# A chain of 3001 GpSimd memsets beside a residual-add and RMSNorm kernel

## The chip, the cores and the metric

The kernel runs on one core of one Trainium2 chip. The metric is the device time of one execution in microseconds (us); lower is better. The median of several is given with its lowest and highest value. The engines are called as the profile calls them: DVE is VectorE, ACT is ScalarE, POOL is GpSimd, SP is SyncE. SPq and ACTq are the queues on which SP and ACT issue transfers.

## The reference

```python
def reference(x, residual, gamma, eps):          # x, residual: (32, 2048, 2048) float32
    z = x + residual
    rms = np.sqrt(np.mean(z ** 2, axis=-1, keepdims=True) + eps)
    return (z / rms * gamma).astype(np.float32)
```

There are 65536 rows of 2048 numbers. Both inputs are read once and the result is written once: 3 x 537 MB = 1611 MB.

## The kernel before

A tile is 7 rows on each of 128 partitions (7168 KB). There are two buffers `z` (x comes in, and the result goes out of the same place) and one area for the residual. Work is spread so: SP loads x and writes the result, ACT loads the residual and sums the squares, DVE adds and scales. GpSimd has nothing to do but the final waits.

```python
    def sp_turn(sp, t):                      # SyncE, one turn
        t.wait(sp, "done", -1)               # the scale of tile i-1 has ended
        inc(sp.dma_start(out=rows(o_f, i - 1), in_=z[(i - 1) % 2]...), "s_out", i - 1)
        ...
        t.wait(sp, "s_out", -1)              # that result has landed: its buffer is free
        ...
            load_x(sp, t, 1)                 # x of tile i+1 into the same buffer

    def dve_turn(v, t, own):                 # VectorE, one turn
        t.wait(v, "x_in"); t.wait(v, "r_in")
        inc(add(v, i, a0, b0), "add_a", i)   # z <- z + r_area, both in SBUF: 128x6144
        inc(add(v, i, a1, b1), "add_b", i)   #                                128x8192
        for h, (a, b) in enumerate(parts(i)):
            ...                              # reciprocal of the rms, after ACT
            ins = scale(v, i, a, b, rstd[p][h])   # z <- z * rstd * gamma_tile (PSUM)
        inc(ins, "done", i)
    ...
    nc.gpsimd.wait_ge(ev["s_out"][(last - 1) % 2], ((last - 1) // 2 + 1) * U)
    nc.gpsimd.wait_ge(s_tail, U * len(tail))
    ...                                      # then GpSimd clears the semaphores
```

(Lines with "..." are cut, and two waits are drawn onto one line.)

Of the kernel before, what the change touches and what calls it, by code (L numbers as in the profile page):

```python
# [9 lines left out]
def kernel(  # L10
# [17 lines left out]
    nc = tc.nc  # L28
    P = nc.NUM_PARTITIONS
# [35 lines left out]
    def sb(name, shape):  # L65
        return ctx.enter_context(nc.sbuf_tensor(name, shape, fp32))
# [6 lines left out]
    def sem(name):  # L73
        sems.append(ctx.enter_context(nc.semaphore(name)))
        return sems[-1]
# [6 lines left out]
    ssq = [[sb(f"ssq{p}{h}", [P, 4]) for h in range(2)] for p in range(2)]  # L82
    rms = [[sb(f"rms{p}{h}", [P, 4]) for h in range(2)] for p in range(2)]
    rstd = [[sb(f"rstd{p}{h}", [P, 4]) for h in range(2)] for p in range(2)]
    tail_ssq = sb("tail_ssq", [P, R])
    tail_rms = sb("tail_rms", [P, R])
    tail_rstd = sb("tail_rstd", [P, R])
# [8 lines left out]
    dve = sem("dve_own")  # L96
    act = sem("act_own")
    s_tail = sem("s_tail")
    tail_ev = {k: sem(f"tail_{k}") for k in ("add", "rms", "done")}


# [115 lines left out]
    def act_part(s, chain, src, a, b, sq, rm):  # L217

        for g in range(a, b):
            if g > a:  # L220
                chain.wait()
            chain.next(
                s.activation(  # L223
                    out=sq_junk[:, :],
                    in_=src[:, g, :],
                    func=Act.Square,
                    accum_out=sq[:, g - a : g - a + 1],
                )
            )
        chain.wait()  # L230
        return s.activation(  # L231
            out=rm, in_=sq[:, : b - a], func=Act.Sqrt, bias=eps_tile[:, :], scale=inv_d
        )

    def act_turn(s, t, chain):
        i, p = t.i, t.p
        for h, (a, b) in enumerate(parts(i)):
            chain.wait()
            t.wait(s, "add_a" if h == 0 else "add_b")
            if h == 0 and i > 0:  # L240
                load_r(s, t, 1)
            inc(
                act_part(s, chain, z[p], a, b, ssq[p][h], rms[p][h][:, : b - a]),
                "rms_a" if h == 0 else "rms_b",
                i,
            )
# [26 lines left out]
    def vector_program(v):  # L273
        v.memset(eps_tile[:, :], float(eps))  # L274
        v.memset(stage, 0.0).then_inc(tail_ev["add"], 1)  # L275
        v.wait_ge(g_in, 4 * U)
        v.stream_shuffle(gamma_tile[:, :].rearrange("p (a b) -> p a b", a=16), stage, [0] * 32)  # L277
        for i in range(LO):
            dve_turn(v, Turn(i), lambda i, h: (2 * i + h + 1) * U)
        with v.Fori(0, 2 * n_iter, 2) as it:  # L280
            for i in range(LO, LO + 2):
                dve_turn(v, Turn(i, it), lambda i, h: it * (2 * U) + (2 * i + h + 1) * U)
        for i in range(HI, last):
            dve_turn(v, Turn(i), lambda i, h: (2 * i + h + 1) * U)
        base = 2 * last * U
        t = Turn(last)
        t.wait(v, "r_in")

        def tail_scale(k):
            a, b = tail[k]  # L290
            v.wait_ge(tail_ev["rms"], k + 1)
            v.reciprocal(out=tail_rstd[:, a:b], in_=tail_rms[:, a:b]).then_inc(dve, U)  # L292
            v.wait_ge(dve, base + (k + 1) * U)
            scale(v, last, a, b, tail_rstd, a).then_inc(tail_ev["done"], 1)

        for k, (a, b) in enumerate(tail):
            v.wait_ge(x_tail[k], U)
            add(v, last, a, b).then_inc(tail_ev["add"], 1)
            if k:
                tail_scale(k - 1)  # L300
        tail_scale(len(tail) - 1)

    def scalar_program(s):
        chain = Chain(s, act)
        for i in range(LO):
            act_turn(s, Turn(i), chain)
        with s.Fori(0, 2 * (n_iter - 1), 2) as it:
            n = chain.n
            chain.base = it * R
            for i in range(LO, LO + 2):  # L310
                act_turn(s, Turn(i, it), chain)
            assert chain.n - n == 2 * R
        chain.base = None
        chain.n = n + 2 * R * (n_iter - 1)
        for i in range(HI - 2, last):
            act_turn(s, Turn(i), chain)
        for k, (a, b) in enumerate(tail):
            chain.wait()
            s.wait_ge(tail_ev["add"], k + 2)
            act_part(  # L320
                s, chain, z[last % 2], a, b, tail_ssq[:, a:b], tail_rms[:, a:b]
            ).then_inc(tail_ev["rms"], 1)

    sync_program(nc.sync)
    vector_program(nc.vector)
    scalar_program(nc.scalar)

    nc.gpsimd.wait_ge(ev["s_out"][(last - 1) % 2], ((last - 1) // 2 + 1) * U)
    nc.gpsimd.wait_ge(s_tail, U * len(tail))
# [38 lines left out]
```

## Time and profile before

| | before |
|---|---|
| time, median of 4 (lowest to highest) | 3724.94 us (3724.76 to 3725.41) |
| transfers | 1610.68 MB, 433 GB/s, DMA engines full |
| DVE, ACT, POOL busy | 62%, 29%, 0% |
| one steady turn (one tile) | 50.8 us |

The groups of instructions, kept apart by shape, give the durations that the argument needs. The columns are line, engine, operation, shapes and count, then total busy us and mean ns of one, then the idle time of the engine before them and what ended it:

```profile
L177 DVE SCALAR_TENSOR_TENSOR z<-z,rstd,gamma_tile 128x2048 f32<-128x2048 f32 x505 | 1153.6, 2344 | 5.2
...
L172 DVE TENSOR_TENSOR z<-z,r_area 128x8192 f32<-128x8192 f32 x72 | 625.3, 8685 | 0.0
L172 DVE TENSOR_TENSOR z<-z,r_area 128x6144 f32<-128x6144 f32 x71 | 465.6, 6558 | 1242.4 <-DMA z<-in_x_dram 1242.4
```

The reader is to see that an add of the larger part takes 8685 ns, that the scales hardly wait, and that DVE's 1242 us of idle time lie where x has not landed yet. The rest of the reading of this profile is in the prediction.

### The profile page before, as it was taken

The numbers are of one execution on the slowest core, as the hardware profiler recorded it, in microseconds if no ns is written. First come the engines' busy times: TensorE is split into PE (matmuls) and PEld (weight loads), VectorE is DVE, ScalarE is ACT, GpSimd is POOL, SyncE is SP. The second block draws the span as 40 slices with busy tenths as digits, with TensorE's granted clock in tenths as the row PEclk, the third lists the DMA queues.
The fourth block names the chain that finished last, engine by engine and source line by source line (L and its number), as shares of the span: only waits on it lengthen the run. The fifth ranks groups of instructions, "written<-read, shape, count | busy, mean of one in ns | idle before, by whom it ended". The sixth has DMA issues, their size and how long they took to land.

```text
span 3723.7 us, 3798 instructions
## 1 busy us (share of the span) xinstructions
DVE 2302.6 (62%) x816; ACT 1072.4 (29%) x1176; POOL 0.2 (0%) x4
## 2 busy tenths in 40 slices
DVE  5666665566665566665566665566665566665566
ACT  2233322233322233322233322233322233322233
POOL 0000000000000000000000000000000000000000
DMA  9999999999999999999999999999999999999999
GB/s 421 431 434 435 434 434 435 434 435 435 434 434 434 434 434 434 434 434 433 434 434 434 434 434 434 434 434 434 434 434 434 434 434 434 434 434 434 434 432 398
DMA packets 32963, 1610.68 MB, mean 433 GB/s; under 512 B 3712, under 2 KB 3776, under 8 KB 3776
## 3 DMA queue, kind: packets, MB, share of 16 engines
q1 hardware_dynamic: 22592, 1082.17, 67.2%
q10 hardware_dynamic: 10368, 528.49, 32.8%
q14 instruction: 3, 0.02, 0.0%
HBM read 1073.77 MB, written 536.87 MB: 433 GB/s over the span
## 4 chain that ended last, share of the span: by engine, by line
DMA 67%; DVE 22%; issue 9%; ACT 2%; SPq 0%; DVEq 0%; ACTq 0%
DMA out_dram<-z 39%; DMA z<-in_x_dram 27%; DVE z L172 15%; DVE z L177 7%; ACT sq_junk L223 1%; ACT rms L231 0%; DVE rstd L197 0%; SPq L259 0%; DVEq L127 0%; DVE r_area L275 0%; ACTq L211 0%; ACTq L127 0%; SPq L141 0%; DVE tail_rstd L292 0%; SPq L162 0%
## 5 line engine op out<-in xcount | busy, mean ns | idle before, releaser
L172 DVE TENSOR_TENSOR z<-z,r_area 128x8192 f32<-128x8192 f32 (+2 forms) x150 | 1109.5, 7437 | 1252.5 <-DMA z<-in_x_dram 1252.5
L223 ACT ACTIVATE sq_junk<-z 128x2048 f32<-128x2048 f32 x512 | 963.4, 1882 | 2617.1 <-DVE z L172 2605.7
L177 DVE SCALAR_TENSOR_TENSOR z<-z,rstd,gamma_tile 128x2048 f32<-128x2048 f32 x505 | 1153.6, 2344 | 5.2
L197 DVE RECIPROCAL rstd<-rms 128x4 f32<-128x4 f32 (+2 forms) x146 | 25.3, 173 | 130.8 <-ACT rms L231 130.8
L223 ACT ACTIVATION_READ_ACCUMULATOR sq_junk<-z 128x1 f32 x512 | 95.5, 186 | 0.0
L231 ACT ACTIVATE rms<-ssq,eps_tile 128x4 f32<-128x4 f32 (+2 forms) x146 | 43.3, 297 | 13.4
L177 DVE SCALAR_TENSOR_TENSOR z<-z,tail_rstd,gamma_tile 128x2048 f32<-128x2048 f32 x7 | 16.2, 2345 | 0.1
L277 DVE LOAD_MASK_SELECT gamma_tile<-r_area x1 | 0.0, 14 | 16.1 <-DMA r_area<-in_gamma_dram 16.1
L277 DVE STREAM_SHUFFLE gamma_tile<-r_area 128x2048 f32<-128x2048 f32 x1 | 2.3, 2290 | 0.0
L275 DVE MEMSET r_area<- 128x2048 f32 x1 | 1.8, 1765 | 0.4 <-issue 0.4
L223 ACT ACT_TABLE_LOAD x1 | 1.3, 1283 | 0.9 <-SPq L77 0.9
L231 ACT ACT_TABLE_LOAD x1 | 1.3, 1283 | 0.1
L231 ACT ACTIVATE tail_rms<-tail_ssq,eps_tile 128x2 f32<-128x2 f32 (+1 forms) x4 | 1.2, 295 | 0.1
L274 DVE MEMSET eps_tile<- 128x1 f32 x1 | 0.1, 59 | 1.0 <-SPq L77 1.0
L292 DVE RECIPROCAL tail_rstd<-tail_rms 128x2 f32<-128x2 f32 (+1 forms) x4 | 0.6, 158 | 0.0
L349 POOL MEMSET const-bfloat16-1.0<- 128x1 bf16 x1 | 0.1, 101 | 0.0
L349 POOL MEMSET const-uint8-127<- 128x1 uint8 x1 | 0.1, 101 | 0.0
L349 POOL MEMSET const-float32-0.0<- 128x1 f32 x1 | 0.1, 98 | 0.2 <-issue 0.2
L349 POOL MEMSET const-float32-1.0<- 128x1 f32 x1 | 0.1, 98 | 0.0
## 6 DMA issues: line engine op xcount, KB each, us to landing
r_area<-in_residual_dram ACTq DMA_DIRECT2D x72, 7168.0 KB, 35.5
z<-in_x_dram SPq DMA_DIRECT2D x71, 7168.0 KB, 27.5
out_dram<-z SPq DMA_DIRECT2D x71, 7168.0 KB, 40.8
z<-in_x_dram SPq DMA_DIRECT2D x3, 2048.0 KB, 17.9
out_dram<-z SPq DMA_DIRECT2D x3, 2048.0 KB, 15.0
r_area<-in_residual_dram SPq DMA_DIRECT2D x1, 5120.0 KB, 25.0
z<-in_x_dram SPq DMA_DIRECT2D x1, 5120.0 KB, 36.7
out_dram<-z SPq DMA_DIRECT2D x1, 5120.0 KB, 26.5
```

The costliest lines, as they stand in the source:

```text
L172: return v.tensor_add(out=s, in0=s, in1=r_area[:, e + a : e + b, :])
L177: ins = v.scalar_tensor_tensor(out=s, in0=s, scalar=rs[:, c + g - a : c + g - a + 1], in1=gamma_tile[:, :], op0=mult, op1=mult,)
L197: v.reciprocal(out=rstd[p][h][:, :n], in_=rms[p][h][:, :n]).then_inc(dve, U)
L223: s.activation(out=sq_junk[:, :], in_=src[:, g, :], func=Act.Square, accum_out=sq[:, g - a : g - a + 1],)
L231: return s.activation(out=rm, in_=sq[:, : b - a], func=Act.Sqrt, bias=eps_tile[:, :], scale=inv_d)
L274: v.memset(eps_tile[:, :], float(eps))
L275: v.memset(stage, 0.0).then_inc(tail_ev["add"], 1)
L277: v.stream_shuffle(gamma_tile[:, :].rearrange("p (a b) -> p a b", a=16), stage, [0] * 32)
L292: v.reciprocal(out=tail_rstd[:, a:b], in_=tail_rms[:, a:b]).then_inc(dve, U)
L349: nc = _bacc.Bacc("TRN2", target_bir_lowering=False, num_devices=1)
```

## The change

It gives GpSimd work that nothing needs. The intent is to learn what a busy GpSimd does to a kernel that does not use it. Every memset waits for the one before it.

```diff
+    scratch = sb("scratch", [P, 1024])
...
+    pool = sem("pool_own")
...
     scalar_program(nc.scalar)
+    nc.gpsimd.memset(scratch[:, :], 0.0).then_inc(pool, 1)
+    with nc.gpsimd.Fori(0, 3000, 8) as it:
+        for k in range(8):
+            nc.gpsimd.wait_ge(pool, it + (k + 1))
+            nc.gpsimd.memset(scratch[:, :], 0.0).then_inc(pool, 1)
+    nc.gpsimd.wait_ge(pool, 3001)
 
     nc.gpsimd.wait_ge(ev["s_out"][(last - 1) % 2], ((last - 1) // 2 + 1) * U)
```

## The prediction

> **What bounds the kernel now.** I read the page's engine shares and slices first, then the chain that ended last, then the timeline of one steady turn, then the GpSimd rows.
>
> The top of the page says that no compute engine is full and the transfers are:
>
> ```profile
> DVE 2302.6 (62%) x816; ACT 1072.4 (29%) x1176; POOL 0.2 (0%) x4
> ...
> DMA  9999999999999999999999999999999999999999
> ...
> DMA packets 32963, 1610.68 MB, mean 433 GB/s; under 512 B 3712, under 2 KB 3776, under 8 KB 3776
> ```
>
> The reader is to see three things: GpSimd (POOL) works 0.2 us, VectorE (DVE) 62% and the 16 DMA engines are at nine tenths or more in every slice. 1610.68 MB at 433 GB/s is 3720 us, the whole span of 3723.7. The stretches view of two steady turns makes it exact:
>
> ```profile
> core 0: us, DVE busy (x) ACT busy (x) POOL busy (x), PEclk, DMA share, GB/s
> 1909.43:1960.24 50.81, 31.41 (x11) 14.61 (x16) 0.00 (x0) 1.00 1.00 433
> 1960.24:2011.06 50.82, 31.41 (x11) 14.61 (x16) 0.00 (x0) 1.00 1.00 433
> ```
>
> The second 1.00 is the DMA share: full. One turn is one tile of three 7168 KB transfers (x in, residual in, result out): 3 x 7.34 MB = 22.02 MB at 433 GB/s = 50.8 us, just what the turn takes. VectorE works 31.4 us of it.
>
> The chain view of the same turns shows what the transfers wait for:
>
> ```profile
> 1891.84 40.80 DMA out_dram<-z
> 1932.66 27.51 DMA z<-in_x_dram
> 1960.24 15.17 DVE z L172 x2
> ```
>
> A result goes out of buffer z (40.8 us), the next x comes into it (27.5), then VectorE adds (15.2) and scales. The chain's 22% on VectorE looks as if VectorE counted. The timeline of one turn says otherwise:
>
> ```profile
> 1909.43 15.16 DVE L172 TENSOR_TENSOR z<-z,r_area 128x6144 f32<-128x6144 f32 x2 [17.62 <-DMA z<-in_x_dram]
> ...
> 1932.66 0.33 SPq L135 DMA_DIRECT2D z<-in_x_dram  x1
> ...
> 1933.50 9.12 DVE L177 SCALAR_TENSOR_TENSOR z<-z,rstd,gamma_tile 128x2048 f32<-128x2048 f32 x4
> 1942.65 0.34 SPq L153 DMA_DIRECT2D out_dram<-z  x1
> 1960.24 15.16 DVE L172 TENSOR_TENSOR z<-z,r_area 128x6144 f32<-128x6144 f32 x2 [17.62 <-DMA z<-in_x_dram]
> ```
>
> VectorE stands 17.62 us idle before each add, waiting for x. And the out transfer issued at 1942.65 stands on the same SyncE queue behind the x load issued at 1932.66, which lands at about 1960.2. So the out transfer's 40.8 us are some 17.6 of queueing and 23.2 of moving. The reader is to see that finishing the scale earlier or later by less than that only changes the time in the queue.
>
> [...]A memset only writes. The trace of before has no overlap of the two engines to test this with. What it can show: the add takes 8685 ns for 8192 elements, 0.94 elements per ns[...], and the scale reads gamma from PSUM, so it has one SBUF stream.
> [...]the constants' memsets read about 100 ns each but start 0.03 to 0.04 us apart, so the rows overlap.
> [...]a residual load (ACT's queue) beside SyncE's queue takes 35.5 us to land, against 7.34 MB / 433 GB/s = 17.0 alone, close to half speed.
>
> ```profile
> 0.23 0.10 POOL L349 MEMSET const-float32-0.0<- 128x1 f32 x1 [0.23 <-issue]
> 0.27 0.10 POOL L349 MEMSET const-float32-1.0<- 128x1 f32 x1
> r_area<-in_residual_dram ACTq DMA_DIRECT2D x72, 7168.0 KB, 35.5
> ```
>
> **The change, part by part.** Nothing is removed; the programs of the other engines keep their instructions and their order. It adds a 4 KB row per partition and, on GpSimd, 1 + 375 x 8 = 3001 memsets of 128x1024 fp32, each waiting for the one before it, and a wait for the last before the old final waits.
>
> *Length of the GpSimd program.* One memset: [...]the fixed 0.10 us that a one-element memset shows, plus the semaphore's way round, 0.03 us between ACT's own chained squares in the timeline[...]. Sum 1.01 to 1.08, so I take 1.05 us.[...] 3001 x 1.05 = 3151 us, or 85% of the run. It starts in the first microseconds, so it ends some 570 us before the last output, and the final wait costs nothing. Break-even is 3724 / 3001 = 1.24 us a memset.
>
> *What it does to VectorE.* [...]Added time: 0. If each of the 150 adds nevertheless waits once for a memset in flight, that is at most 2 x 1.05 = 2.1 us a turn, against a reserve of 17.6 us. With fair sharing instead of a queue in order the reserve would be smaller: at 1942.65 the residual has 9.0 us to go at a third of the rate (3.0), x 9.0 at a third and 8.5 at half (7.3), so 10.3 us of full-rate work lie ahead before the DMA engines would run dry. So VectorE may lose 10 to 17 us in each of 72 turns, 720 us or more in all, before the end moves.
>
> *What it does to the transfers.* They are all on hardware queues of SyncE and ACT, none on GpSimd, and bytes do not change. Added time: 0.
>
> *Path sum.* 3724.9 + 0 + 0[...]. I write 3726.
>
> **The rivals.**
> A. *GpSimd becomes the bound because a memset is longer than 1.24 us.* At 1.35 us the end is 3001 x 1.35 = 4051 us, 9% slower; at 1.28, 3841, 3% slower. Against it: my terms need another 0.19 us each. For it: the fixed cost of a large memset with a chained semaphore is measured nowhere in this trace, and the loop has a branch every eight memsets. I give it 7%.
> B. [...]Then memsets cannot run under the adds, 15.2 us of every 50.8. By 3724 us, 70% x 3724 / 1.05 = 2480 memsets would be done; the other 521 would run alone after the outputs, 547 us, so about 4270 us, 15% slower. VectorE itself would lose 2.1 us a turn, hidden. [...]I give it 5%.
> C. *The writes take SBUF bandwidth from the transfers.* 3001 x 0.52 MB = 1573 MB of added writes, as many bytes as the transfers move. The DMA engines are at 1.00, so this is the one place where 1% costs 1% (37 us) at once. Against it: [...]VectorE and ACT already pass more than that beside 433 GB/s. I give a visible loss of over 2% only 2%.
> D. *It gets faster.* Nothing is removed from the full resource; under 1%.
>
> **Range and chances.** If no rival holds, only the noise of the runs (0.2 us between three) and a small loss by C remain: 3720 to 3740. About 14% of the chance lies in A to C; the top of the range takes in a small case of C or a bare case of A (1.25 us gives 3751). So 3718 to 3760 holds eight in ten. Chances: faster by over 2% 0.01, within 2% 0.86, slower by over 2% 0.13.
>
> **What would show each step right or wrong.** *Length:* GpSimd memsets spaced 1.0 to 1.1 us start to start, the last one at 3000 to 3250 us, and slices of zero after that. If GpSimd is busy to the last slice and ends the chain, A or B holds. *A against B:* under A the spacing is the same all along; under B it stretches in the windows of the adds and is short elsewhere. *VectorE:* the mean of the 128x8192 add stays at 8685 ns and of the scale at 2344; if they grow, there is contention, and VectorE's wait for x (17.6 us a turn) must shrink by as much with the time unchanged. *Transfers:* DMA share 1.00 and 433 GB/s in steady windows, turns of 50.8 us; a lower rate with longer turns is C. The prediction is wrong if the spacing is above 1.24 us for any reason, or if the rate of the transfers falls.

Its sums need a word:

- One memset came to 1.01 to 1.08 us and was taken as 1.05. Of the terms, 0.10 us (the one-element memset) and 0.03 us (ACT's chained squares) stand. Measured afterwards: 854, 98 and 57 ns (experiment 3).
- The path sum came to 3726 us: 3724.9 + 0 + 0, and an allowance of under 1 us for the set-up of the added program, which is a guess.
- The zero for VectorE rested on a rule. The trace of before could not show it; the runs do (adds of 8685 ns in both kernels). Rival B is the case that memsets can't run while an add runs. The chances of B and C were judgement.
- That VectorE and ACT already pass more bytes than the memsets is an estimate from shapes and times: the adds and scales of one tile alone read and write 5 x 7.34 = 36.7 MB of SBUF in a turn of 50.8 us, and memsets of 0.524 MB every 1.05 us would write 25.4 MB. The 17.0 us of a residual load alone is an estimate too, its bytes over the rate of all transfers.

## The result, and the profile after

| | before | after |
|---|---|---|
| time, median of 4 (lowest to highest) | 3724.94 us (3724.76 to 3725.41) | 3732.89 us (3731.45 to 3734.54) |
| ratio, 95% interval | | 1.0021 (1.0004 to 1.0039) |
| profiled span | 3723.7 us | 3731.7 us |

The ratio here and below is taken over the fast runs that both kernels had in the same rounds, so it is not quite the ratio of the medians quoted beside it. The interval leaves 1 out, and no run of after is as short as the longest of before: the changed kernel is some 8 us slower.

The top of the page of the changed kernel:

```profile
DVE 2302.6 (62%) x816; ACT 1072.5 (29%) x1176; POOL 2854.4 (76%) x3005
...
POOL 9999999999999999999999999999999940000000
DMA  9999999999999999999999999999999999999999
...
DMA packets 32963, 1610.68 MB, mean 432 GB/s; under 512 B 3712, under 2 KB 3776, under 8 KB 3776
```

POOL is busy for 33 of the 40 slices and then has nothing; DVE's 2302.6 us are the same to the tenth; the transfers move the same bytes at 432 instead of 433 GB/s. Its groups by shape, in the columns explained above:

```profile
L333 POOL MEMSET scratch<- 128x1024 f32 x3000 | 2853.2, 951 | 172.0
L179 DVE SCALAR_TENSOR_TENSOR z<-z,rstd,gamma_tile 128x2048 f32<-128x2048 f32 x505 | 1153.6, 2344 | 5.2
...
L174 DVE TENSOR_TENSOR z<-z,r_area 128x8192 f32<-128x8192 f32 x72 | 625.3, 8685 | 0.0
L174 DVE TENSOR_TENSOR z<-z,r_area 128x6144 f32<-128x6144 f32 x71 | 465.7, 6559 | 1249.5 <-DMA z<-in_x_dram 1249.5
```

The adds and scales have not moved by more than 1 ns. The view of the memset's line adds the shortest, the median and the longest, and the first and the last start:

```profile
L333 POOL MEMSET scratch<- x3000: 951/951/954, 2.0 to 3026.2; 128x1024 f32 x188
```

3000 memsets lie within 3 ns of each other, whether an add runs beside them or not, and start (3026.2 - 2.0) / 2999 = 1.008 us apart. Last, the stretches of two steady turns, and the same turn in the timeline:

```profile
1912.99:1963.92 50.93, 31.41 (x11) 14.61 (x16) 48.06 (x51) 1.00 1.00 432
1963.92:2014.84 50.92, 31.41 (x12) 14.62 (x16) 48.00 (x52) 1.00 1.00 432
```

```profile
1912.99 15.16 DVE L174 TENSOR_TENSOR z<-z,r_area 128x6144 f32<-128x6144 f32 x2 [17.74 <-DMA z<-in_x_dram]
...
1937.05 9.12 DVE L179 SCALAR_TENSOR_TENSOR z<-z,rstd,gamma_tile 128x2048 f32<-128x2048 f32 x4
1946.20 0.34 SPq L155 DMA_DIRECT2D out_dram<-z  x1
1963.92 6.56 DVE L174 TENSOR_TENSOR z<-z,r_area 128x6144 f32<-128x6144 f32 x1 [17.75 <-DMA z<-in_x_dram]
```

The turn has the same shape, but it is 50.92 us long where the turns shown of before have 50.81. All of the difference is in the wait for x: 17.74 against 17.62 us. So the time is lost in the transfers, a tenth of a us at a time. Lining up the first add of every turn of the two traces (turn n is tile n + 1, and its length is the time since the entry of turn n - 1) shows where:

```
turn         3       14      15      32       33       59       69       last 128x4096 add   end of span
before    182.79  741.09  791.84  1654.71  1706.17  3027.33  3535.40         3690.30          3723.7
after     182.77  741.10  792.01  1657.70  1709.32  3033.41  3541.62         3697.63          3731.7
after -    -0.02    0.01    0.17     2.99     3.15     6.08     6.22            7.33             8.0
```

The numbers are the start of that add in us. Up to turn 14 nothing is lost, although the memsets run from the start. Then every turn takes 0.16 us more (50.92 instead of 50.76). From turn 33 on, where the kernel before itself steps from 50.76 to 50.82 us, the surplus is 0.11 us. At turn 60 the memsets have ended (the last one starts at 3026 us) and the surplus is gone: 0.14 us in the next ten turns. Another 1.8 us come after turn 69, when GpSimd is already idle, so not all of the 8 us fall while memsets run.

### The profile page after: what moved, and what is told of

It reads as the page before. It is cut to its first block, busy times and chain, and to the rows that moved or that the text cites. A ratio compares the mean times of both kernels' runs of the same rounds, so it can differ in the third digit from the quotient of the medians.

```text
span 3731.7 us, 10550 instructions
## 1 busy us (share of the span) xinstructions
DVE 2302.6 (62%) x816; ACT 1072.5 (29%) x1176; POOL 2854.4 (76%) x3005
## 2 busy tenths in 40 slices
DMA packets 32963, 1610.68 MB, mean 432 GB/s; under 512 B 3712, under 2 KB 3776, under 8 KB 3776
## 4 chain that ended last, share of the span: by engine, by line
DMA 67%; DVE 22%; issue 9%; ACT 2%; SPq 0%; DVEq 0%; ACTq 0%
DMA out_dram<-z 39%; DMA z<-in_x_dram 27%; DVE z L174 15%; DVE z L179 7%; ACT sq_junk L225 1%; ACT rms L233 0%; DVE rstd L199 0%; SPq L261 0%; DVEq L129 0%; DVE r_area L277 0%; ACTq L213 0%; ACTq L129 0%; SPq L143 0%; DVE tail_rstd L294 0%; SPq L164 0%
## 5 line engine op out<-in xcount | busy, mean ns | idle before, releaser
L333 POOL MEMSET scratch<- 128x1024 f32 x3000 | 2853.2, 951 | 172.0
L179 DVE SCALAR_TENSOR_TENSOR z<-z,rstd,gamma_tile 128x2048 f32<-128x2048 f32 x505 | 1153.6, 2344 | 5.2
L233 ACT ACTIVATE rms<-ssq,eps_tile 128x4 f32<-128x4 f32 (+2 forms) x146 | 43.3, 297 | 13.4
L329 POOL MEMSET scratch<- 128x1024 f32 x1 | 1.0, 951 | 0.5 <-PEq L371 0.5
## 6 DMA issues: line engine op xcount, KB each, us to landing
z<-in_x_dram SPq DMA_DIRECT2D x1, 5120.0 KB, 36.7
```

Source lines behind the costliest of these rows:

```text
L179: ins = v.scalar_tensor_tensor(out=s, in0=s, scalar=rs[:, c + g - a : c + g - a + 1], in1=gamma_tile[:, :], op0=mult, op1=mult,)
L233: return s.activation(out=rm, in_=sq[:, : b - a], func=Act.Sqrt, bias=eps_tile[:, :], scale=inv_d)
L329: nc.gpsimd.memset(scratch[:, :], 0.0).then_inc(pool, 1)
L333: nc.gpsimd.memset(scratch[:, :], 0.0).then_inc(pool, 1)
```

## The experiments

Twelve runs were made. All gave the reference's output. The kernel before was timed again beside each set, with medians from 3724.87 to 3725.53 us.

### 1. The changed kernel once more; the kernel before once more

No edit. Is the small excess real, and does it belong to the memsets?

> The changed kernel unchanged, once more. Question: is the excess of about 8 us (0.2%) over the kernel before real, and is it tied to a place in the run? Theory (memsets cost the transfers a little): 3730 to 3735 us again, turns of 50.92 us instead of 50.82 in the stretch from about 1700 to 3027 us, and turns of 50.81 us as soon as the memsets have ended. Rival (drift between executions): anything from 3725 to 3735, and the longer turns do not end where the memsets end.

> The kernel before, unchanged, for a second trace of it. Theory (the longer turns belong to the memsets): turns of 50.76 us up to turn 32 and 50.82 from turn 33 on, no onset of anything longer, span near 3724 us. Rival (the longer turns start by chance in any execution, late in the first third): a stretch of 50.9 us turns here too.

The changed kernel took 3732.72 us (3731.14 to 3733.77, 5 runs; ratio 1.0020, interval 1.0006 to 1.0033). The kernel before took 3725.38 us (3724.71 to 3725.92, 4 runs; ratio 0.9999). In the repeat, the turns are about 50.76 us until turn 21 (but for turns 4 and 7, of 51.08 and 51.02) and 50.92 from turn 23 on, and they fall back to 50.80 to 50.84 us when the memsets end at turn 60, until the last one (51.82). In the second trace of before every add starts within 0.04 us of the first trace from turn 3 to 32 and within 0.53 us up to turn 69. Its rival shows faintly: turns 38 to 40, 60 and 61 are 50.86 to 50.91 us long with no memset in the program, but no such stretch lasts. None of the changed kernel's nine executions (3731.14 us or more) is as short as the longest of before in any set (3726.70). So the excess belongs to the memsets. Where it sets in differs (turn 15 in one execution, turn 22 in another of the same program), so it isn't tied to one tile.

### 2. The same memsets of one partition

```diff
-    nc.gpsimd.memset(scratch[:, :], 0.0).then_inc(pool, 1)
+    nc.gpsimd.memset(scratch[0:1, :], 0.0).then_inc(pool, 1)
     ...                                  # and the same in the loop
```

> The same 3001 memsets with the same semaphore chain, but of one partition of 1024 elements instead of 128, so the same instructions at the same spacing (1.008 us expected, as the time goes by elements in a partition) with 1/128 of the bytes written. Theory S (the written bytes cost the transfers the 0.1 to 0.16 us a turn): the time falls back to 3725 us and turns to 50.76 to 50.82 us. Rival I (the instructions, semaphores or their records cost it): it stays at 3731 to 3734 us.

3732.63 us (3732.22 to 3735.38, 5 runs; ratio 1.0020, interval 1.0006 to 1.0034). The view of the memset's line (shortest, median and longest, first and last start):

```profile
L333 POOL MEMSET scratch<- x3000: 941/941/944, 2.0 to 2996.3; 1x1024 f32 x188
```

One memset reads 941 ns, against 951 with all 128 partitions, at a spacing of 0.998 us. The turns are about 50.92 us from turn 16 on, as with all 128 partitions. With 1/128 of the bytes the excess is the same: theory S has fallen. The written bytes are not what the transfers lose time to. The profiled execution is the longest of the five (3735.38 us): it lost some 4 us more in turns 60 to 64 (up to 52.43 us), after the last memset.

### 3. Half as many, nearly three times as many, and a quarter of the semaphore steps

```diff
 # half: a bf16 row of the same 4 KB, 1505 memsets of 128x2048
+    scratch = ctx.enter_context(nc.sbuf_tensor("scratch", [P, 2048], mybir.dt.bfloat16))
+    with nc.gpsimd.Fori(0, 1504, 8) as it:
 # short: 8001 memsets of 128x256
+    with nc.gpsimd.Fori(0, 8000, 8) as it:
+            nc.gpsimd.memset(scratch[:, :256], 0.0).then_inc(pool, 1)
 # quarter: four one-byte rows of 1024, one wait and one increment for four memsets
+            nc.gpsimd.wait_ge(pool, it + (k + 1))
+            for m in range(4):
+                ins = nc.gpsimd.memset(scratch[:, m, :], 0)
+            ins.then_inc(pool, 1)
```

(Only the main lines of each edit are shown; the first memset, the loop's count and the final wait change to match.)

> 1505 memsets of 128x2048 bf16 in place of 3001 of 128x1024 fp32: the same 4 KB row, but half as many instructions, waits and increments over about the same time[...] (spacing about 1.86 us, end at about 2800 us). Theory I (each instruction, with its semaphores, costs the transfers a little): half the excess, 3728 to 3730 us, turns of 50.84 to 50.87 us. Rival (any activity on GpSimd sets a fixed turn of 50.92): 3732 us again.

> 8001 memsets of 128x256 fp32 in place of 3001 of 128x1024: spacing about 0.37 us[...], so 2.7 times as many instructions and semaphore steps in a us, over about 2950 us. Theory I (cost per instruction): the excess of a turn grows to 0.3 or 0.4 us, the time to 3740 to 3750 us. Rival (fixed turn of 50.92 whatever the rate): 3732 us.

> 3004 memsets of 128x1024 one-byte elements in disjoint rows, but only every fourth waits and increments, so the instructions stay about as many in a us (spacing 0.9 to 1.0 us) and the semaphore steps fall to a quarter. Theory Sem (the semaphore steps cost it): about a quarter of the excess, 3727 us. Theory Rec (the instructions themselves, or the records that the profiler writes of them, cost it): 3731 to 3734 us. Also: without the wait each time the spacing should fall from 1.008 to about 0.9 us, which says what the chain costs.

The spacing is (last start - first start) / (count - 1) of the line view. "Turn" is the usual length of a turn with the loss, in turns 23 to 32, where the kernel before has 50.76.

| kernel | spacing, us | median time, us (range) | ratio, interval | turn, us |
|---|---|---|---|---|
| half as many | 1.863 | 3729.21 (3727.61 to 3730.20) | 1.0009 (0.9996 to 1.0023) | 50.87 |
| quarter of the semaphore steps | 0.918 | 3730.37 (3729.51 to 3730.70) | 1.0012 (0.9999 to 1.0026) | 50.88 |
| the change | 1.008 | 3732.89 (3731.45 to 3734.54) | 1.0021 (1.0004 to 1.0039) | 50.92 |
| 128x256, short | 0.368 | 3755.32 (3746.67 to 3761.14) | 1.0079 (1.0065 to 1.0092) | 51.1, some 51.5 to 51.7 |

A fixed turn of 50.92 us is refuted: among these chained memsets the loss grows with the rate of the instructions. Half the rate costs 3729.21 - 3725.31 = 3.9 us, the change 8 us, 2.7 times the rate 30 us. The last is more than in proportion, and more than the 3740 to 3750 us expected: the usual surplus of a turn is 0.36 us, as expected, but some turns lose 0.7 to 0.9. The two smaller ratios have intervals that reach 1, so for these two it is the turns in the trace that show it rather than the ratios, though none of their executions is as short as the longest of before beside them (3726.47 us). The third edit answers its question only by half: with a quarter of the waits and increments 5.1 us of the 8 remain, neither a quarter nor all. It also removes three quarters of the register additions that compute the next wait. Which of the three (memset, semaphore step, addition) costs how much is not settled.

The three sizes also give the law of one memset. Their line views, and that of the quarter run, read:

```profile
L333 POOL MEMSET scratch<- x8000: 311/311/314, 1.3 to 2948.0; 128x256 f32 x196
```

```profile
L333 POOL MEMSET scratch<- x1504: 1804/1805/1807, 2.8 to 2802.2; 128x2048 bf16 x188
```

```profile
L336 POOL MEMSET scratch<- x3000: 951/952/956, 4.6 to 2759.0; 128x1024 uint8 x188
```

From 256 to 1024 elements it is (951 - 311) / 768 = 0.833 ns an element, from 1024 to 2048 (1805 - 951) / 1024 = 0.834, and 98 ns are left over as the fixed part. (The terms of the 0.37 us expected of the short memset, with these figures and the 57 ns from one memset's end to the next start in the change, 1.008 - 0.951, are 0.214 + 0.098 + 0.057 = 0.369 us, and 0.368 was measured.) Two-byte elements cost as much as four-byte ones, and 1024 one-byte elements (952 ns) as much as 1024 of four bytes.

### 4. Copies instead of memsets

GpSimd now reads SBUF as well.

```diff
+    scratch2 = sb("scratch2", [P, 512])
-            nc.gpsimd.memset(scratch[:, :], 0.0).then_inc(pool, 1)
+            nc.gpsimd.tensor_copy(out=scratch2[:, :], in_=scratch[:, :512]).then_inc(pool, 1)
```

> 3000 copies of 128x512 fp32 on GpSimd from one scratch row into another in place of the memsets: now GpSimd reads SBUF as well. [...]Theory[...]: copies take about 0.6 us each outside VectorE's adds, and stand still or wait under the adds (15.2 us of every 50.8), so the mean spacing grows to 0.8 us or more and GpSimd ends at 2400 to 2700 us; VectorE's adds may wait up to one copy. Rival (there is no sharing at all here): even spacing of about 0.6 us, end at about 1800 us. In both the kernel's time stays within 2% of 3725 us, since VectorE has 17 us a turn to spare.

The time is 3727.68 us (3727.08 to 3729.33, 4 runs; ratio 1.0008, interval 0.9993 to 1.0023). The line view of the copies and the adds by shape:

```profile
L334 POOL COPY scratch<-scratch x3000: 609/613/8953, 2.0 to 2845.5; 128x512 f32<-128x512 f32 x188
```

```profile
L175 DVE TENSOR_TENSOR z<-z,r_area 128x8192 f32<-128x8192 f32 x72 | 648.1, 9002 | 0.0
L175 DVE TENSOR_TENSOR z<-z,r_area 128x6144 f32<-128x6144 f32 x71 | 475.7, 6700 | 1210.4 <-DMA z<-in_x_dram 1210.4
```

A copy takes 613 ns in the middle and up to 8953, a whole add. The stretches view of one turn, with GpSimd's busy time and count, shows when (the first stretch is under the adds, the second under the scales and the wait for x):

```profile
1911.00:1926.00 15.00, 14.94 (x2) 1.00 0.99 428
1927.00:1960.00 33.00, 29.96 (x50) 1.00 1.00 431
```

Two copies in 15 us under the adds, fifty in the next 33. A copy that reads SBUF stands still while an add with two SBUF inputs runs; the view counts the standing still as busy. Beside the scales, which have one SBUF input, it does not: 14 copies from 1929.58 us on, most of them under scales, take 9.39 us in all, and 15 from 1944.44 us on, when the scales have ended and DVE waits for x, take 10.06 us; both start 0.675 us apart. And the add pays a little: 9002 instead of 8685 ns in the mean, and 9097 ns for the longest between 1000 and 2500 us, 412 ns more, which is less than one copy. The last copy starts at 2845 us, later than the 2400 to 2700 expected, at a mean spacing of 0.948 us. All this is hidden, as DVE's idle time before the adds shrank from 1242 to 1210 us.

This run also limits what experiment 3 found. It has as many instructions, waits, increments and additions as the change, slightly closer together, and yet it costs 3727.68 - 3724.87 = 2.8 us where the repeat of the change, beside the same runs of before, costs 7.9. Its turns 23 to 32 are 50.85 us, not 50.92. So the loss is not one fixed price for each instruction, semaphore step or record: the kind of instruction, or how it is spread over the turn, matters too.

### 5. 4001 memsets

```diff
-    with nc.gpsimd.Fori(0, 3000, 8) as it:
+    with nc.gpsimd.Fori(0, 4000, 8) as it:
...
-    nc.gpsimd.wait_ge(pool, 3001)
+    nc.gpsimd.wait_ge(pool, 4001)
```

> 4001 memsets instead of 3001. Theory (spacing 1.008 us; GpSimd is a second path that runs beside the transfers and only its end counts): the last memset ends at 2 + 4001 x 1.0083 = 4036 us, the kernel takes 4037 to 4042 us, 8% over the kernel before, the outputs being done at about 3730 us. Rival (memsets and transfers are in each other's way for longer, so both stretch): over 4060 us, or outputs done later than 3745 us.

4038.34 us (4038.32 to 4038.35, 4 runs; ratio 1.0841, interval 1.0824 to 1.0857). The chain that ended last, which was 67% transfers in the other two kernels, is now on GpSimd:

```profile
POOL 82%; issue 14%; POOLq 4%; SPq 0%
```

The other engines ended nearly on time: the last scale starts at 3715.96 us, 9.5 us later than the 3706.46 before, and the last output is issued at 3718.3 us. By the 14.3 us that it takes to land in the changed kernel it lands at about 3733 us (an estimate), where about 3730 had been expected. So the two paths run side by side, and the longer one sets the time.

### 6. How much VectorE has to spare

```diff
+    idle = sb("idle", [P, 2, 16])
...
         inc(add(v, i, a1, b1), "add_b", i)
+        for k in range(7 if t.it is not None else 0):      # 10 in the other run
+            v.tensor_reduce(
+                out=idle[:, p, k : k + 1], in_=gamma_tile[:, :],
+                axis=mybir.AxisListType.X, op=mybir.AluOpType.add,
+            )
```

These are on the kernel before, without memsets.

> The kernel before with 7 reductions of gamma (PSUM, 128x2048, about 2.3 us each, results unused) on VectorE between add and scale, in the 70 turns of the loop: 16 us more VectorE work a turn, 1.7 of it inside the wait for ACT, so the scale ends some 14.5 us later. This tests the reserve of the prediction. Theory (queue in order: the out transfer stands behind x anyway, reserve 17.6 us): time within 2 us of 3725, out transfer 40.8 - 14.5 = 26 us to landing, VectorE idle before the adds 3 us a turn. Rival (fair sharing, reserve 10.3 us): 4 us a turn more, about 4010 us.

> The same with 10 reductions, 23 us more VectorE work a turn, 21.3 us beyond the wait for ACT. Theory (reserve 17.6 us): VectorE becomes the bound, 3.7 us a turn too much, 70 x 3.7 = 260 us, about 3985 us, VectorE busy 95% or more in the loop. Rival (reserve 10.3 us): 11 us a turn, about 4495 us.

With seven: 3743.50 us (3742.24 to 3744.44, 4 runs; ratio 1.0048, interval 1.0031 to 1.0064). With ten: 3948.64 us (3947.68 to 3950.56, 4 runs; ratio 1.0597, interval 1.0580 to 1.0615). The timeline of one turn with seven, and then one with ten:

```profile
1915.24 0.34 SPq L154 DMA_DIRECT2D out_dram<-z  x1
1919.39 15.16 DVE L173 TENSOR_TENSOR z<-z,r_area 128x6144 f32<-128x6144 f32 x2 [4.18 <-issue]
1934.47 15.47 DVE L196 TENSOR_REDUCE idle<-gamma_tile 128x1 f32<-128x2048 f32 x7
1942.92 0.33 SPq L136 DMA_DIRECT2D z<-in_x_dram  x1
```

```profile
2020.12 15.15 DVE L173 TENSOR_TENSOR z<-z,r_area 128x6144 f32<-128x6144 f32 x2
2020.23 0.34 SPq L154 DMA_DIRECT2D out_dram<-z  x1
2026.85 0.34 ACTq L142 DMA_DIRECT2D r_area<-in_residual_dram  x1
2035.19 22.06 DVE L196 TENSOR_REDUCE idle<-gamma_tile 128x1 f32<-128x2048 f32 x10
```

With seven, the out transfer lands 1942.92 - 1915.24 = 27.7 us after its issue instead of 40.8, and DVE waits 4.2 us before the add instead of 17.6. So 13.1 to 13.4 us of later scale were taken out of its time in the queue. With ten, DVE goes from the scales straight into the next add in the turn shown; in every other turn it still waits about 1.3 us there (44.4 us over 34 turns). So DVE is very nearly the bound. The surplus is (3948.64 - 3725.53) / 70 = 3.2 us a turn. The added work is 22.06 us a turn, of which 1.70 fill the old wait for ACT. So 22.06 - 1.70 - 3.2 = 17.2 us were free, which is the 17.6 of the queue in order and not the 10.3 of fair sharing. The reductions started 2.21 us apart where 2.3 had been assumed: 22.06 instead of 23 us a turn takes 66 us off the 3985 expected, and the 17.2 in place of 17.6 puts some 30 back. The 18 us of the run with seven are not explained: 2 had been expected, and the rival wanted 285. The DMA engines show full there too, at 431 GB/s over the span. Its turns scatter from 50.75 to 51.93 us with nothing on GpSimd, so somewhat longer turns are not peculiar to a busy GpSimd; whether the cause is the same is not shown.

### 7. Memsets and copies where VectorE is the bound

The ten reductions together with the change, and together with the copies.

> The ten reductions a turn together with the 3001 memsets of the change: VectorE is the bound (98.7% busy in the run with ten reductions, 3948.6 us), so anything that memsets do to VectorE shows in the time one for one, and the small loss of the transfers hides. Theory (a writer does not meet VectorE's adds): 3947 to 3951 us, adds at 8684 and 6555 ns. Rival (each add waits for the memset in flight): up to half a memset, 0.5 us, for each of 150 adds, 4000 to 4030 us. (Against the run with ten reductions, not the kernel before.)

> The ten reductions a turn together with the 3000 copies, which do wait for the adds and the adds for them. Theory[...]: in the run of copies alone the adds grew by 34 us in all over some 56 turns; here they cost that one for one, 3975 to 3990 us, copies again up to 8.9 us long under an add. Rival (adds that wait are hidden even here): 3949 us.

With memsets: 3947.13 us (3947.12 to 3948.25, 4 runs), against 3948.64 without. With copies: 3963.05 us (3962.33 to 3964.03, 4 runs). These are compared with the earlier set of runs, on another chip, whose time of the kernel before (3725.53 us) was within 0.5 us of this set's (3725.06). The adds by shape, first with the ten reductions alone, then with memsets, then with copies:

```profile
L173 DVE TENSOR_TENSOR z<-z,r_area 128x8192 f32<-128x8192 f32 x72 | 625.2, 8684 | 0.0
L173 DVE TENSOR_TENSOR z<-z,r_area 128x6144 f32<-128x6144 f32 x71 | 465.4, 6555 | 71.2 <-issue 44.4 <-DMA z<-in_x_dram 26.8
```

```profile
L175 DVE TENSOR_TENSOR z<-z,r_area 128x8192 f32<-128x8192 f32 x72 | 625.3, 8685 | 0.0
L175 DVE TENSOR_TENSOR z<-z,r_area 128x6144 f32<-128x6144 f32 x71 | 465.5, 6556 | 67.5 <-issue 41.0 <-DMA z<-in_x_dram 26.4
```

```profile
L176 DVE TENSOR_TENSOR z<-z,r_area 128x8192 f32<-128x8192 f32 x72 | 646.1, 8974 | 0.0
L176 DVE TENSOR_TENSOR z<-z,r_area 128x6144 f32<-128x6144 f32 x71 | 471.2, 6636 | 54.2 <-issue 28.7 <-DMA z<-in_x_dram 24.7
```

Even with hardly anything to spare, 3001 memsets cost DVE nothing (the rival wanted 4000 us or more), and the loss of the transfers is hidden. Copies do cost: the adds grew by 646.1 - 625.2 + 471.2 - 465.4 = 26.7 us over the run without copies, of which 14.4 us reached the time. The forecast of 26 to 41 us missed, as it took the growth of the run with copies alone one for one; DVE still had some 70 us of waiting before its adds, and that fell to 54.

## Why the prediction was right

**Length of the GpSimd program: right.** The spacing is 1.008 us against 1.05, and the last memset starts at 3026 us, inside the 3000 to 3250 named. Of its terms, the fixed 0.10 us holds: 0.834 ns an element (854 for the row) and 98 ns fixed make the 951 ns of the row. From its end to the next start 57 ns pass, where ACT's chained squares had given 0.03 us. The break-even of 1.24 us was the right thing to check: with 1000 memsets more, the kernel was 8.4% slower (experiment 5). Rival A is therefore a real mechanism, which this count of memsets stays clear of.

**VectorE: right, and shown.** The adds (8685 ns) and scales (2344 ns) are unchanged beside 3000 memsets. The rule from which the prediction took its zero is cut; the zero itself is what was measured. (One reading is loose: the 17.62 us of waiting stand before the first add of each turn, not before each add.) Rival B is true of a reader and false of a writer: the copies stood still under the adds as B described (up to 8953 ns), and the memsets did not vary by more than 3 ns (951 to 954).

**The reserve: right in size.** Of the two figures given, 17.6 and 10.3 us, the chip decided for the queue in order, at 17.2 us. But the end moved before the reserve was used up: with some 13.4 us of it gone, the kernel was already 18 us slower (0.26 us a turn), which the prediction did not foresee and no run explains.

**The transfers: the step that missed by a little.** The prediction says "Added time: 0" for them. The measured term is 8 us, or 0.2%. The prediction also said that it would be wrong if the rate of the transfers fell. By that sign of its own this step failed: 433 GB/s became 432, and turns of 50.81 us became 50.92. The total stayed inside the range, which had been made wide enough for a small case of rival C. But C's reason was wrong: not the bytes written (1/128 of them cost the same) but something that grows with the rate of the memsets and is smaller with copies at the same rate. Three things stay open. It isn't known which step of an instruction costs it. It isn't known why the loss sets in only after 400 to 1150 us. And it isn't known whether the loss comes of the recording: every execution reported here also has its span and clock listed, so there is no execution that is known to be free of records.

## What to carry to other kernels

Before you price work on an idle engine, find the resource that is full and ask whether the added work uses it; here the DMA engines were full (share 1.00 in steady turns) and the memsets didn't use them (1610.68 MB before and after), so 2854 us of busy time cost 8. Then compare the length of the new program with the span: 3001 memsets ended within it, and 4001 were the last to end and made it 4038 us. And ask whether GpSimd reads or only writes SBUF: here copies stopped for VectorE's adds with two SBUF inputs (613 ns in the middle, up to 8953), and memsets did not (951 to 954 ns).
